# Building the output matrix of a chunked delta rule later, between the splits of a weight stream

## The chip, the cores and the metric

The kernel runs on one core of a Trainium2 chip. The metric is the device time of one execution in microseconds (us); three executions of the kernel before gave 1591.21, 1593.24 and 1593.59 us.

## The reference

One decoder layer for 256 prompt tokens and 8 sequences of 4 sample tokens, everything in fp32. What matters here:

```python
proj = x @ w_in                                  # 2048 -> 11280 columns, split in parts
y_a  = (gB * conv3(gC * h)) @ w_a_out            # mixer A
q, k, v = silu(conv4(q|k|v))                     # mixer B, 8 heads of 128
q, k = l2norm(q), l2norm(k)
# gated delta rule, chunks of 64 tokens, per head:
decay = exp(gcum_i - gcum_j)  where j <= i       # gcum: running sum of g within the chunk
M     = strict_lower(beta * (k k^T) * decay)
T     = inverse(I + M)
attn  = (q k^T) * decay                          # the matrix for the outputs
v_new = T(beta v) - T(beta k exp(gcum)) S
o     = (q exp(gcum)) S + attn v_new
S     = S exp(glast) + (k exp(glast - gcum))^T v_new
y_b   = (rmsnorm(o) * silu(z)) @ w_b_out
x = LN(ALPHA * x + (sigmoid(m_a) * y_a + sigmoid(m_b) * y_b) @ w_o)
x = LN(ALPHA * x + relu(x @ w_up)^2 @ w_down)    # 2048 -> 8192 -> 2048
```

## The kernel before, in words

**The weight stream.** All weights (266 MB) pass once through the core in blocks of 512 KB (`blocks`, some 500 of them). Each block is loaded by SP's queue into a buffer `raw`, split by ACT into a rounded part `hi` (`split_hi`, L194) and by DVE into the rest `lo = raw - hi` (`split_lo`, a subtraction recorded by the helper at L149), and used by PE in 24 matmuls of 288 columns (`matmuls`, L215): for every 128 rows and 128 columns one of the high part of x with `hi`, one of its low part (`xl`, `dl`, `hl`) with `hi`, one of the high part with `lo`. `raw`, `hi` and `lo` have four buffers each. A block's `hi` and `lo` are made three blocks ahead (two in the first ten), and its `raw` is asked for seven ahead, as soon as the `lo` that read the same buffer last is done.

**Order.** There is no scheduler: each engine works in the order in which the program was written. The main loop goes over the blocks; in each it writes the `hi` of block i+3, one step of the side work, `lo` of block i+3, the evacuations that are due (dictionary `due`), and then the 24 matmuls. So DVE and ACT reach the side step of a block in the same order as their splits, and whatever waits in a step has the next splits queued behind it.

**The side work** is a generator, one `yield` per block. `gdn(0)` and then `gdn(1)` run the delta rule for heads 0 to 3 and 4 to 7 (called the first and the second delta rule below). A step's names: `gl`, `glx` are the decays and their split for the running sums; `E` is `decay`; `nr` and `rn` the norms of k and their reciprocals; `nM` (in the buffer `gl`) is -M; `aT` is the matrix for the outputs, `E` times q k^T; `mx` the diagonal 8x8 blocks; `U` the inverse, built from them by a chain of small DVE operations (L1408 to L1416), a transpose, and small 32x32 matmuls (L1399). The decay needs an exponential (L1306) and the norms a root (L1314) on ACT. `kq` products lie in two PSUM tiles of a pool of four (`gtile`) until `nM` and `aT` have read them. Then the chunks c = 0 to 3 follow: L1571 (state times q and k), L1583 (`v`), L1596 and L1599 (new state and outputs), with extra empty steps for the first delta rule. A second generator (`aux`, `sample`) steps along in the same blocks for the sample tokens. POOL's queue loads the sample states of two heads (`states_in(2)`, `states_in(3)`, 512 KB each) in the step that makes `mx`.

**The start.** x comes token by token and is turned by PE transposes, 128 columns at a time; the last quarter of the prompt goes over DVE and POOL instead (`x_turn`, `x_moves`, `x_last`). `x_sample(3)` turns the last quarter of the sample tokens: a transpose put among the matmuls of block 5, a copy on ACT (`xh`), a subtraction on DVE (`xl`). Block 6 is the first that needs that quarter.

**The first down projection** (`mark["down", 0]`, 16 blocks): each pair of blocks ends in `acc += psum` on DVE (`down_evac`), which also frees one of the two PSUM accumulators. In the same blocks pieces of the normalised x are split (`normal`, whose `parts` makes `dl`); they were entered in `due` before the evacuations.

Of the kernel before, what the change touches and what calls it, by code (L numbers as in the profile page):

```python
# [110 lines left out]
def hybrid_kernel(ctx: ExitStack, tc: tile.TileContext, A):  # L111
# [105 lines left out]
    def matmuls(i):  # L217
        gi, r0, k0, first, last = blocks[i]
        if gi.get("by_token"):
            return first_tokens(i, k0)  # L220
        members = gi.get("pair", (gi,))
        if first:
            for m in members:
                m["ps"] = acp.tile([P, 2, 512], F32, tag="acc", name=nm("acc"))
        ps = members[0]["ps"]
        h, l = his.pop(i), los.pop(i)
        ah, al = gi["acts"]()
        n = gi["width"]
        kb = gi["kb"]
        h, l = (u.rearrange("p k c -> p (k c)").rearrange("p (k c) -> p k c", k=kb) for u in (h, l))  # L230
        for k in range(kb):
            xh_, xl_ = ah[:, k0 + k, 0:n], al[:, k0 + k, 0:n]
            st = first and k == 0
            en = last and k == kb - 1
            per = gi["cols"] // P // len(members)
            for u, m in enumerate(members):
                ts = [(m["ps"][:, t, 0:n], slice((per * u + t) * P, (per * u + t + 1) * P)) for t in range(per)]
                both = [(o, c, x) for o, c in ts for x in (xh_, xl_)]
                behind = i == mark["down", 0] + 1 and k > 1
                for o, c, x in both[::2] if behind else both[::2] + both[1::2] if i == 0 else both:  # L240
                    stream(o, h[:, k, c], x, start=st and x is xh_, stop=False)
                for o, c in ts:
                    stream(o, l[:, k, c], xh_, start=False, stop=en and not behind)
                    if fill:
                        fill.pop(0)()
                for o, c, x in both[1::2] if behind else ():
                    stream(o, h[:, k, c], x, start=False, stop=en)
        if last:
            for n, f in enumerate(gi["evac"]):
                at(i + 1 + n, lambda f=f: f(ps))  # L250


    NE, NL = CF_AT["early"], CF_AT["late"]
# [939 lines left out]
    def gdn(G):  # L1193
# [59 lines left out]
        def move_sums(s):  # L1253
            for b in range(2):
                for i in range(4):
                    gps.tensor_copy(red4[64 * s + 32 * b:64 * s + 32 * b + 32, i].rearrange("p (c r) -> p c r", r=2),
                                    ptv[32 * i:32 * i + 32, 1 - s, b])

        for n in range(4):
            for f, hh in ((total, n - 2), (square, n - 1), (turn, n)):  # L1260
                if hh >= 0:
                    f(hh)
            if n != 1 or G == 0:
                yield
        total(2)
        square(3)
        tt(gl, bc(G_["g"][:, :, pr], 64),
           cst("lc").unsqueeze(1).unsqueeze(1).to_broadcast([P, 4, 2, 64]), MUL)
        gps.memset(aT, 0.0)
        glf = gl.rearrange("p c r x -> p (c r x)")  # L1270
        glx = pl.tile([P, 2, 512], F32R, tag="vml", name=nm("glx"))
        act.copy(glx[:, 0], glf)
        yield
        tt(glx[:, 1], glf, glx[:, 0], SUB)
        total(3)
# [27 lines left out]
        act.copy(kr, sp2[:, 0:P])  # L1303
        move_k(gps.tensor_copy, 1, 0)
        yield
        act.activation(Ef, Ef, AF.Exp)  # L1306

        for u, q4, par, r in halves:
            tt(Tm[r, q4], kk2[u][r, :, par], bmid(ident[r, 64 * par:64 * par + 64], 4), MUL)
        dve.tensor_reduce(out=ss[:, 0:8], in_=Tm, axis=mybir.AxisListType.X, op=ADD)  # L1310
        yield
        nr = T([P, 9], "nr")
        rn = T([P, 9], "rn")
        act.activation(nr, ss[:, 0:9], AF.Sqrt, bias=epsc[:, 1:2])  # L1314
        move_sums(0)
        yield
# [7 lines left out]
        stt(nbr, brk, -1.0, rk, MUL, MUL)  # L1324
        nM = T([P, 8, 64], "gl")
        tt(nM, Ef, bc(qc(nbr), 64), MUL)
        tt(Ef, Ef, bc(rn[:, 0:8], 64), MUL)
        for u, q4, par, r in halves:
            tt(nM[r, q4], kk2[u][r, :, par], nM[r, q4], MUL)
        yield  # L1330
        for u, q4, par, r in halves:
            tt(aT[r, q4, 64 - 64 * par:128 - 64 * par], kk2[u][r, :, 1 - par], Ef[r, q4], MUL)

        n8 = sqr[:, 0:64].rearrange("p (q j) -> p q j", q=8)
        u8 = sqr[:, 64:128].rearrange("p (q j) -> p q j", q=8)
        t8 = sqr[:, 128:192].rearrange("p (q j) -> p q j", q=8)
# [58 lines left out]
        def pairs(out, a, b):  # L1395
            for q in range(8):
                for w in range(4):
                    r = slice(32 * w, 32 * w + 32)
                    pe.matmul(out[r, q * 32:q * 32 + 32], a(r, q, w), b[r, q, :], start=True, stop=True)  # L1399

        yield
        n88 = gtile()
        for u in range(2):
# [162 lines left out]
        for c in range(4):  # L1566
            blk, half = c // 2, c % 2
            if c:
                p1 = gtile().rearrange("p (h x) -> p h x", h=4)
                for hh in range(4):  # L1570
                    pe.matmul(p1[:, hh, :], kq[:, hh, c].rearrange("p s x -> p (s x)"), S[:, hh, :],  # L1571
                              start=True, stop=True)
                for hh in range(4):
                    r = rows[hh % 2]
                    stt(v[r, c, hh // 2, :], p1[r, hh, :], G_["neg"][r, c, 2 * G + hh // 2:2 * G + hh // 2 + 1],
                        v[r, c, hh // 2, :], MUL, ADD)
                for par in range(2):
                    r = rows[1 - par]
                    tt(o[r, c], p1[r, par::2, :], bc(G_["egs"][r, c, pr], P), MUL)
                yield  # L1580
            p2 = gtile()
            for p in range(2):
                pe.matmul(p2[:, p * P:(p + 1) * P], U128[:, 2 * c + p, :], v[:, c, p, :], start=True, stop=True)  # L1583
            tt(v[:, c], p2[:, 0:256].rearrange("p (r x) -> p r x", r=2), bc(brk[:, c, :], P), MUL)
            if c == 0:
                kdf = kdec.rearrange("p c r x -> p (c r) x")
                tt(kdf, kdf, bc(qc(kdr), P), MUL)
                dve.tensor_reduce(out=ss[:, 9:17], in_=red4.rearrange("p i n -> p n i"), axis=mybir.AxisListType.X,
                                  op=ADD)
            yield  # L1590
            if c == 0 or G == 0:
                yield
            p3, p4 = [gtile()[:, 0:256].rearrange("p (h c) -> p h c", h=2) for _ in range(2)], gtile()
            for hh in range(4):
                r = rows[hh % 2]
                pe.matmul(p3[hh % 2][:, hh // 2, :], kdec[r, c, hh // 2, :], v[r, c, hh // 2, :],  # L1596
                          start=True, stop=True)
            for p in range(2):
                pe.matmul(p4[:, p * P:(p + 1) * P], aT[:, 2 * c + p, :], v[:, c, p, :], start=True, stop=True)  # L1599
            p4v = p4[:, 0:256].rearrange("p (r x) -> p r x", r=2)  # L1600
            if c == 0:
                for par in range(2):
                    act.copy(S[:, par::2, :], p3[par])
                act.copy(o[:, c], p4v)
            else:
                for hh in range(4):
                    stt(S[:, hh, :], S[:, hh, :], G_["egl"][:, blk, 4 * G + hh, half:half + 1],
                        p3[hh % 2][:, hh // 2, :], MUL, ADD)
                tt(o[:, c], o[:, c], p4v, ADD)
            yield  # L1610
            if G == 0 and c < 2:
                yield
        gps.dma_start(A["new_gdn_prompt"][0, 0, hs].rearrange("h d e -> d h e"), S)
        while not done:
# [113 lines left out]
    for i in range(len(blocks)):  # L1728
# [7 lines left out]
        if i in (1, 3):  # L1736
            a_, s_, b_ = x_fill(i // 2 + 1)
            fill.extend([idle, a_, s_, b_])
        if i == 5:
            fill.extend([idle, idle, lambda: x_sample(3)()])  # L1740
        if i == 6:
            fill.extend([idle, idle, idle, idle, hist_tiles, hist_tiles2])
# [115 lines left out]
```

## Time and profile before

| | before |
|---|---|
| three runs, median (range) | 1593.24 us (1591.21 to 1593.59) |
| the profiled execution's own time | 1591.5 us |
| its span, first to last instruction | 1589.4 us |
| granted TensorE clock | 0.999 |
| PE busy in the span | 1580.8 us |
| DVE busy | 979.2 us |
| ACT busy | 783.6 us |

A row of the timeline has the start in us, the length in us, the engine, the source line, the operation, what it writes and reads, how many instructions the row merges, and in brackets how long the engine sat idle before it and for whom. `SPq` and `POOLq` are issues of transfers. Lengths of neighbouring instructions overlap, since they are pipelined: the step from one start to the next is what an instruction costs its engine.

### The profile page before, as it was taken

To read this page: it belongs to the slowest core of one execution; us is meant where nothing else is said; L and a number is where in the kernel's file an instruction comes from. 1 tells how busy PE (TensorE), PEld (TensorE's weight loads), DVE (VectorE), ACT (ScalarE), POOL (GpSimd) and SP (SyncE) were. 2 spreads that over 40 slices of the span, in tenths; PEclk is the share of its full clock that TensorE was granted. 3 is DMA by queue.
4 is the path that set the end of the run, shared out by engine and by line. 5 is a ranking of instruction groups with operands and counts; after the bars stand their busy time and mean duration, and the time that the engine had idled before them with its cause. 6 is when DMAs were issued, how large, how long until landed. Compare 5 with 4: busy or idle time off the path is not lost.

```text
span 1589.4 us, 31399 instructions
## 1 busy us (share of the span) xinstructions
PE 1580.8 (99%) x13125; PEld 1565.2 (98%) x13125; DVE 979.2 (62%) x1301; ACT 783.6 (49%) x1231; POOL 133.0 (8%) x278
## 2 busy tenths in 40 slices
PE   9999999999999999999999999999999999999998
PEld 8999999999999999999999999999999999999997
DVE  6787788777544455557888755445445544445566
ACT  6786777458533344444456544334334443344454
POOL 1142316133000000000000000000000000000111
PEclk9999999999999999999999999999999999999999
DMA  8666467645755556655555755555555555555653
GB/s 268 176 186 187 135 181 211 188 127 157 224 172 174 173 172 174 177 174 170 168 159 174 235 178 173 173 172 173 172 173 173 174 174 174 174 174 176 188 170 104
DMA packets 273236, 280.42 MB, mean 176 GB/s; under 512 B 13727, under 2 KB 267220, under 8 KB 272832
## 3 DMA queue, kind: packets, MB, share of 16 engines
q1 hardware_dynamic: 269190, 266.06, 55.4%
q0 software_dynamic: 3616, 12.02, 2.8%
q8 instruction: 103, 1.69, 0.5%
q10 hardware_dynamic: 288, 0.33, 0.1%
q14 instruction: 39, 0.32, 0.1%
HBM read 270.88 MB, written 7.48 MB: 175 GB/s over the span
## 4 chain that ended last, share of the span: by engine, by line
PE 93%; ACT 2%; DVE 2%; issue 1%; POOL 0%; DVEq 0%; ACTq 0%
PE acc L215 90%; ACT hi L194 1%; DVE lo L149 1%; DVE w L152 0%; PE g L1399 0%; PE g L1596 0%; PE g L1599 0%; PE g L1571 0%; PE g L1390 0%; PE g L1583 0%; PE g L1549 0%; DVE gl L149 0%; ACT L321 0%; ACT vm L1538 0%; PE g L1094 0%
## 5 line engine op out<-in xcount | busy, mean ns | idle before, releaser
L149 DVE TENSOR_TENSOR lo<-raw,hi 128x1024 fp32r<-128x1024 f32 (+1 forms) x503 | 606.5, 1210 | 512.6 <-ACT hi L194 511.4
L194 ACT CAST hi<-raw 128x1024 fp32r<-128x1024 f32 (+1 forms) x499 | 517.9, 1042 | 654.2 <-PE acc L215 579.0
L215 PE MATMUL acc<-xh,hi 128*128 128x288 f32 x1408 | 385.5, 291 | 0.3 <-ACT xh L1008 0.2
L215 PE MATMUL acc<-xl,hi 128*128 128x288 f32 x1408 | 381.7, 289 | 0.3 <-DVE xl L149 0.3
L215 PE MATMUL acc<-xh,lo 128*128 128x288 f32 x1408 | 294.4, 289 | 0.7 <-DVE lo L149 0.6
L215 PE MATMUL acc<-dl,hi 128*128 128x288 f32 (+1 forms) x1024 | 278.4, 289 | 0.0
L215 PE MATMUL acc<-dh,hi 128*128 128x288 f32 (+1 forms) x1024 | 278.2, 288 | 0.0
L215 PE MATMUL acc<-hh,hi 128*128 128x288 f32 x992 | 268.2, 288 | 0.1
L215 PE MATMUL acc<-hl,hi 128*128 128x288 f32 x992 | 268.2, 288 | 0.0
L215 PEld LDWEIGHTS acc<-xh,hi 128*128 128x128 f32 x1408 | 264.3, 188 | 3.1 <-issue 1.6
L215 PEld LDWEIGHTS acc<-xl,hi 128*128 128x128 f32 x1408 | 264.9, 188 | 1.4 <-DVE xl L149 0.5
L215 PEld LDWEIGHTS acc<-xh,lo 128*128 128x128 f32 x1408 | 222.0, 188 | 1.5 <-DVE lo L149 1.5
L215 PE MATMUL acc<-dh,lo 128*128 128x288 f32 (+1 forms) x1024 | 213.5, 288 | 0.0
L215 PE MATMUL acc<-hh,lo 128*128 128x288 f32 x992 | 206.0, 288 | 0.0
L215 PEld LDWEIGHTS acc<-dl,hi 128*128 128x128 f32 x1024 | 192.4, 188 | 0.0
L215 PEld LDWEIGHTS acc<-dh,hi 128*128 128x128 f32 x1024 | 191.6, 187 | 0.0
L215 PEld LDWEIGHTS acc<-hl,hi 128*128 128x128 f32 x992 | 186.4, 188 | 0.0
L215 PEld LDWEIGHTS acc<-hh,hi 128*128 128x128 f32 x992 | 185.4, 187 | 0.7 <-issue 0.4
L215 PEld LDWEIGHTS acc<-dh,lo 128*128 128x128 f32 x1024 | 161.1, 188 | 0.0
L215 PEld LDWEIGHTS acc<-hh,lo 128*128 128x128 f32 x992 | 155.6, 188 | 0.0
L215 PE MATMUL acc<-mh,hi 128*128 128x288 f32 x256 | 69.2, 288 | 0.0
L215 PE MATMUL acc<-ml,hi 128*128 128x288 f32 x256 | 69.2, 288 | 0.0
(429 smaller groups left out, 1470.9 us busy)
## 6 DMA issues: line engine op xcount, KB each, us to landing
raw<-in_w_in_dram SPq DMA_DIRECT2D x175, 512.0 KB, 4.0
raw<-in_w_up_dram SPq DMA_DIRECT2D x128, 512.0 KB, 3.6
raw<-in_w_down_dram SPq DMA_DIRECT2D x128, 512.0 KB, 3.6
raw<-in_w_o_dram SPq DMA_DIRECT2D x32, 512.0 KB, 4.4
raw<-in_w_a_out_dram SPq DMA_DIRECT2D x16, 512.0 KB, 3.6
raw<-in_w_b_out_dram SPq DMA_DIRECT2D x16, 512.0 KB, 3.6
S<-in_state_gdn_dram POOLq DMA_DIRECT2D x8, 512.0 KB, 5.5
out_dram<-S POOLq DMA_DIRECT2D x8, 512.0 KB, 4.7
```

The lines of the kernel that those rows point to most:

```text
L149: dve.tensor_tensor(out=out, in0=a, in1=b, op=op)
L194: act.copy(his[i][:, k:k + step], raw[i][:, k:k + step])
L215: pe.matmul(out, w, x, **kw)
```

## The change

Five edits, none of which adds or removes an operation of the program's own.

1. `aT` and the product `E * rn` that it needs move from the two steps after the norms to the step just before the matmul with `bo8` (L1404), in both delta rules.
2. The exponential moves one step later, to stand directly ahead of the root.
3. In the second delta rule the decays (`gl` and the high half of `glx`) are made one step earlier.
4. In the first delta rule one empty step moves from behind chunk 1 to between L1571 and L1583 of chunk 3, so that all from the end of chunk 1 to L1571 of chunk 3 comes one block earlier.
5. `x_sample(3)` goes to block 4, and in the first down projection the evacuation stands at the head of its block's `due` list.

```diff
@@ matmuls
             for n, f in enumerate(gi["evac"]):
-                at(i + 1 + n, lambda f=f: f(ps))
+                due.setdefault(i + 1 + n, []).insert(
+                    0 if mark["down", 0] <= i < mark["down", 0] + 16 else 9999, lambda f=f: f(ps))
@@ gdn
+        glf = gl.rearrange("p c r x -> p (c r x)")
+        glx = pl.tile([P, 2, 512], F32R, tag="vml", name=nm("glx"))
+
+        def decays():
+            tt(gl, bc(G_["g"][:, :, pr], 64),
+               cst("lc").unsqueeze(1).unsqueeze(1).to_broadcast([P, 4, 2, 64]), MUL)
+            act.copy(glx[:, 0], glf)
+
         for n in range(4):
             ...
+            if G and n == 3:
+                decays()
             if n != 1 or G == 0:
                 yield
         total(2)
         square(3)
-        tt(gl, bc(G_["g"][:, :, pr], 64), ...)
+        if G == 0:
+            decays()
         gps.memset(aT, 0.0)
-        glf = ...
-        glx = ...
-        act.copy(glx[:, 0], glf)
@@ gdn
         yield
-        act.activation(Ef, Ef, AF.Exp)
-
         for u, q4, par, r in halves:
             tt(Tm[r, q4], kk2[u][r, :, par], bmid(ident[r, 64 * par:64 * par + 64], 4), MUL)
         dve.tensor_reduce(out=ss[:, 0:8], in_=Tm, axis=mybir.AxisListType.X, op=ADD)
         yield
         nr = T([P, 9], "nr")
         rn = T([P, 9], "rn")
+        act.activation(Ef, Ef, AF.Exp)
         act.activation(nr, ss[:, 0:9], AF.Sqrt, bias=epsc[:, 1:2])
@@ gdn
         tt(nM, Ef, bc(qc(nbr), 64), MUL)
-        tt(Ef, Ef, bc(rn[:, 0:8], 64), MUL)
         for u, q4, par, r in halves:
             tt(nM[r, q4], kk2[u][r, :, par], nM[r, q4], MUL)
         yield
-        for u, q4, par, r in halves:
-            tt(aT[r, q4, 64 - 64 * par:128 - 64 * par], kk2[u][r, :, 1 - par], Ef[r, q4], MUL)
...
+        tt(Ef, Ef, bc(rn[:, 0:8], 64), MUL)
+        for u, q4, par, r in halves:
+            tt(aT[r, q4, 64 - 64 * par:128 - 64 * par], kk2[u][r, :, 1 - par], Ef[r, q4], MUL)
         yield
         n88 = gtile()
@@ gdn, chunks
                 yield
+                if G == 0 and c == 3:
+                    yield
             p2 = gtile()
...
-            if G == 0 and c < 2:
+            if G == 0 and c == 0:
                 yield
@@ main loop
-        if i == 5:
+        if i == 4:
             fill.extend([idle, idle, lambda: x_sample(3)()])
```

How the order changes, at three places. First ACT in the first delta rule, before: the exponential stands between a split and the SiLU of v (`vf`, `vfs`), the root one split further down.

```order
L194 CAST hi_1382<-raw_1226 128x1024
L1306 ACT_TABLE_LOAD
L1306 ACTIVATE E_1334<-E_1334 128x512
L321 ACT_TABLE_LOAD
L321 ACTIVATE vf_501<-w_494 128x4x64
L323 ACTIVATE vfs_502<-w_494 128x32
L321 ACTIVATE vf_501<-w_495 128x4x64
L323 ACTIVATE vfs_502<-w_495 128x32
L194 CAST hi_1422<-raw_1262 128x1024
L1314 ACT_TABLE_LOAD
L1314 ACTIVATE nr_1424<-ss_966,epsc 128x9
```

And the same place after:

```order
L194 CAST hi_1382<-raw_1226 128x1024
L322 ACTIVATE vf_501<-w_494 128x4x64
L324 ACTIVATE vfs_502<-w_494 128x32
L322 ACTIVATE vf_501<-w_495 128x4x64
L324 ACTIVATE vfs_502<-w_495 128x32
L194 CAST hi_1421<-raw_1262 128x1024
L1320 ACT_TABLE_LOAD
L1320 ACTIVATE E_1334<-E_1334 128x512
L1321 ACT_TABLE_LOAD
L1321 ACTIVATE nr_1423<-ss_966,epsc 128x9
```

The exponential went behind the next split, and the table load ahead of the SiLU is gone: two loads are left of three.

Second, ACT in the second delta rule, before, where no SiLU lies between the two:

```order
L194 CAST hi_3710<-raw_3568 128x1024
L1306 ACT_TABLE_LOAD
L1306 ACTIVATE E_3671<-E_3671 128x512
L194 CAST hi_3746<-raw_3604 128x1024
L1314 ACT_TABLE_LOAD
L1314 ACTIVATE nr_3748<-ss_3418,epsc 128x9
L194 CAST hi_3787<-raw_3642 128x1024
```

After:

```order
L194 CAST hi_3710<-raw_3568 128x1024
L194 CAST hi_3745<-raw_3604 128x1024
L1320 ACT_TABLE_LOAD
L1320 ACTIVATE E_3671<-E_3671 128x512
L1321 ACT_TABLE_LOAD
L1321 ACTIVATE nr_3747<-ss_3418,epsc 128x9
L194 CAST hi_3787<-raw_3642 128x1024
```

Here the exponential and its table load stand behind the second split instead of ahead of it; as many loads as before.

Third, DVE in the first delta rule from `nM` on, before (the second delta rule has the same order, with its own numbers):

```order
L149 TENSOR_TENSOR gl_1475<-E_1334,nbr_1472 128x512
L149 TENSOR_TENSOR E_1334<-E_1334,rn_1425 128x512
L149 TENSOR_TENSOR gl_1475<-g_1315,gl_1475 64x256 x2
L149 TENSOR_TENSOR gl_1475<-g_1316,gl_1475 64x256 x2
L149 TENSOR_TENSOR lo_1482<-raw_1305,hi_1463 128x1024
L149 TENSOR_TENSOR aT_961<-g_1315,E_1334 64x4x64 x2
L149 TENSOR_TENSOR aT_961<-g_1316,E_1334 64x4x64 x2
L149 TENSOR_TENSOR xt_1333<-gl_1475,cf 128x512
L149 TENSOR_TENSOR lo_1520<-raw_1380,hi_1513 128x1024
```

After, four splits further down, where the product with `rn` and `aT` now stand:

```order
L149 TENSOR_TENSOR mx_1587<-xt_1333,mx_1587 128x512
L149 TENSOR_TENSOR lo_1628<-raw_1510,hi_1625 128x1024
L149 TENSOR_TENSOR w_494<-acc_1485,hs_1483 128x2x256
L149 TENSOR_TENSOR w_494<-acc_1485,hs_1483 128x8x4 x2
L149 TENSOR_TENSOR E_1334<-E_1334,rn_1424 128x512
L149 TENSOR_TENSOR aT_961<-g_1315,E_1334 64x4x64 x2
L149 TENSOR_TENSOR aT_961<-g_1316,E_1334 64x4x64 x2
L149 TENSOR_TENSOR lo_1672<-raw_1541,hi_1663 128x1024
L152 SCALAR_TENSOR_TENSOR w_495<-w_494,hwa,w_495 128x304 x4
L1414 COPY vmh_959<-cf 128x64
```

The five operations passed five splits (`lo` 1481, 1515, 1557, 1597, 1628) and now stand between the gate product `w` of mixer A and the split ahead of the chain that builds `U`.

More of the change, by code (lines that the diff above doesn't have):

```diff
@@ L1266, in gdn @@
         square(3)
-        tt(gl, bc(G_["g"][:, :, pr], 64),
-           cst("lc").unsqueeze(1).unsqueeze(1).to_broadcast([P, 4, 2, 64]), MUL)
+        if G == 0:
+            decays()
         gps.memset(aT, 0.0)
-        glf = gl.rearrange("p c r x -> p (c r x)")
-        glx = pl.tile([P, 2, 512], F32R, tag="vml", name=nm("glx"))
-        act.copy(glx[:, 0], glf)
         yield
```

## The prediction

> **What bounds the kernel now.** I read the page first, then the chain of waits, then PE's timeline, and last those of DVE and ACT at the places where PE waits.
>
> ```profile
> PE 1580.8 (99%) x13125; PEld 1565.2 (98%) x13125; DVE 979.2 (62%) x1301; ACT 783.6 (49%) x1231; POOL 133.0 (8%) x278
> 394.61 325.28 PE acc L215 x2568
> ```
>
> PE is busy for 1580.8 of 1589.4 us. The second row, from the chain of waits, gives its pace without any side work: 325.28 / 2568 = 127 ns for a matmul, so 3.05 us for a block of 24. No edit touches a matmul. The most that can be won is what PE waits, so every wait of PE that lies near an edit has to be priced. From PE's timeline:
>
> ```profile
> 29.18 0.29 PE L215 MATMUL acc<-xh,hi 128*128 128x288 f32 x1
> 29.75 0.40 PE L215 MATMUL acc<-xl,hi 128*128 128x288 f32 x1 [0.28 <-DVE xl L149]
> 113.78 0.40 PE L215 MATMUL acc<-xh,lo 128*128 128x288 f32 x1 [0.25 <-DVE lo L149]
> 117.40 0.39 PE L215 MATMUL acc<-xh,lo 128*128 128x288 f32 x1 [0.31 <-DVE lo L149]
> 120.44 0.29 PE L215 MATMUL acc<-xl,hi 128*128 128x288 f32 x1
> 120.81 0.39 PE L215 MATMUL acc<-xh,lo 128*128 128x288 f32 x1
> 218.59 0.38 PE L1583 MATMUL g<-v,U 128*128 128x128 f32 x1 [0.20 <-DVE v L152]
> 871.82 0.41 PE L215 MATMUL acc<-hh,lo 128*128 128x288 f32 x2
> 872.34 0.37 PE L215 MATMUL acc<-hh,hi 128*128 128x288 f32 x1
> ```
>
> The reader is to see that a wait costs more than the gap in brackets: from 29.18 to 29.75 are 0.57 us where 0.13 would do, so a gap of 0.28 costs 0.44, 0.16 more than it shows. With the same 0.16 the gaps at 113.78 and 117.40 cost 0.41 and 0.47. At 120.81 the step is 0.37 instead of 0.13, a loss of 0.25 (rounded up from unrounded starts). At 218.59 it is about 0.3 (0.20 to 0.36). At 872.34 the second of the pair started at 871.95, so the loss is 0.27. All together 2.1 us, 0.13% of the time: the prize is that small.
>
> **The x of the sample tokens.**
>
> ```profile
> 26.14 1.14 ACT L1054 CAST xh<-xm 128x512 fp32r<-128x512 f32 x2 [0.47 <-POOL xm L1049]
> 28.27 1.23 DVE L149 TENSOR_TENSOR lo<-raw,hi 128x1024 fp32r<-128x1024 f32 x1 [0.18 <-ACT hi L194]
> 29.41 0.28 DVE L149 TENSOR_TENSOR xl<-g,xh 128x128 fp32r<-128x128 f32 x1
> ```
>
> PE waits for the `xl` that ends at 29.69, and that one stood behind the split of 28.27. A block earlier, its copy fits into ACT's idle 0.47 before 26.14, and the subtraction runs with DVE idle. What is late next is the `lo` of block 6: it ends at 29.50, and PE asks for it five matmuls into the block, at 29.18 + 4 x 0.127 = 29.69. Gain 0.44, and no less than 0.25 by that margin if the split slips by the length of the small operation. SP's transfers keep their order.
>
> **The first delta rule.**
>
> ```profile
> 101.85 1.28 ACT L1306 ACT_TABLE_LOAD   x1
> 103.78 1.28 ACT L321 ACT_TABLE_LOAD   x1
> 108.64 0.21 DVE L1318 RECIPROCAL rn<-nr 128x9 f32<-128x9 f32 x1 [0.39 <-ACT nr L1314]
> 110.02 0.69 DVE L149 TENSOR_TENSOR E<-E,rn 128x512 f32<-128x512 f32 x1
> 112.50 1.23 DVE L149 TENSOR_TENSOR lo<-raw,hi 128x1024 fp32r<-128x1024 f32 x1
> 113.76 1.73 DVE L149 TENSOR_TENSOR aT<-g,E 64x256 f32<-64x256 f32 x4
> 121.00 1.05 ACT L194 CAST hi<-raw 128x1024 fp32r<-128x1024 f32 x1 [0.72 <-DMA raw<-in_w_in_dram]
> 122.87 1.22 DVE L149 TENSOR_TENSOR lo<-raw,hi 128x1024 fp32r<-128x1024 f32 x1
> 126.13 1.22 DVE L149 TENSOR_TENSOR lo<-raw,hi 128x1024 fp32r<-128x1024 f32 x1 [1.00 <-ACT hi L194]
> 135.31 0.45 DVE L1416 STREAM_TRANSPOSE U<-U 128x256 f32<-128x256 f32 x1
> 136.18 0.31 PE L1399 MATMUL g<-U,gl 32*32 32x32 f32 x13
> ```
>
> First the root. Without the exponential ACT saves 1.93 us (101.85 to 103.78) and the SiLU's table load of 1.28. It then waits for DVE's last convolution piece, and pays 1.28 and some 0.65 for the exponential behind the next split. By hand the norms come within 0.1 us of 108.6, so DVE starts `rn` as before.
>
> Then the splits. The `lo` of 112.50 loses `E * rn` ahead of it (0.69) and ends at about 113.05; PE's lost 0.41 says that it wanted it at 113.37. The next ones have 0.69 + 1.73 = 2.4 us less ahead of them, against losses of 0.47 and 0.25. All three waits go: gain 1.13 us. The 2.4 us turn up ahead of the `lo` of 126.13, where DVE sat idle for 1.00.
>
> What is late next is `U`. From 108.64 to the end of the transpose (135.76) DVE has 27.12 us, of which 1.00 idle, so 26.12 of work. If that idle is filled by `aT`, `U` ends at 108.7 + 26.1 = 134.8. PE comes 1.13 earlier than 136.18, at 135.05, and needs 0.05 us after the release (113.73 to 113.78). It just fits, with 0.2 to spare. This asks that the weight load which ACT awaited at 121.00 land earlier too: it is asked for when the `lo` of 112.50 ends, 0.7 us sooner, and the sample states of two heads are on their way then. If it landed at the same time, DVE, which reaches the `lo` of 122.87 about 2.35 us sooner and found its `hi` ready for 0.82, would idle for 1.5, and `U` would cost PE 1.3. I take 0, for this reason:
>
> ```profile
> 111.77 1.76 POOL L1201 DMA_DIRECT2D S<-in_state_gdn_dram  x2 [14.04 <-ACT kdec L1250]
> 279.63 1.77 POOL L1201 DMA_DIRECT2D S<-in_state_gdn_dram  x2 [7.10 <-ACT hs L345]
> DMA to landing us min/median/max: 7.1/7.1/7.1
> DMA to landing us min/median/max: 5.4/5.4/5.4
> ```
>
> The two landings are those of the weight loads asked for at 113.75 and at 280.73. The one came 1.1 us after the second state load (issued halfway through the POOL row, at 112.65) and took 7.1 us; the other came 0.2 after it and took 5.4. After the change the first stands at 113.05, 0.4 behind, near the quick one: landing at about 118.5 to 119.
>
> [...]
>
> **The chunks.**
>
> ```profile
> 199.15 0.54 DVE L152 SCALAR_TENSOR_TENSOR w<-w,hw 128x312 f32<-128x312 f32 x1 [2.17 <-ACT w L311]
> 217.08 1.46 DVE L152 SCALAR_TENSOR_TENSOR v<-g,gpt,v 64x128 f32<-64x128 f32 x4
> ```
>
> PE waited at 218.59 for the `v` of 217.08. With an empty step between them it has a block more. The same four operations of chunk 2 go a block earlier, into the idle 2.17 ahead of 199.15. PE has 12 blocks with side matmuls there before and after, so the entries cost the same. Gain 0.3.
>
> **The decays of the second delta rule.**
>
> ```profile
> 91.92 0.72 PE L1285 MATMUL g<-glx,hmr 128*128 128x512 f32 x2
> 263.99 0.96 PE L1285 MATMUL g<-glx,hmr 128*128 128x512 f32 x2
> ```
>
> The same two matmuls take 0.24 more there, because they catch up with DVE's `glx`. A product less ahead of it gives that back: 0 to 0.24, and I take 0.24.
>
> **The down projection.** The evacuation goes ahead of one split of `dl`, which nobody reads before the next up projection. PE's 0.27 at 872.34 goes.
>
> **The second delta rule**, where the same moves cost.
>
> ```profile
> 270.95 1.28 ACT L1306 ACT_TABLE_LOAD   x1
> 272.92 1.05 ACT L194 CAST hi<-raw 128x1024 fp32r<-128x1024 f32 x1
> 275.62 0.21 DVE L1318 RECIPROCAL rn<-nr 128x9 f32<-128x9 f32 x1 [0.39 <-ACT nr L1314]
> 275.96 1.05 ACT L194 CAST hi<-raw 128x1024 fp32r<-128x1024 f32 x1 [0.37 <-PE acc L215]
> 293.13 1.23 DVE L149 TENSOR_TENSOR lo<-raw,hi 128x1024 fp32r<-128x1024 f32 x1 [1.00 <-ACT hi L194]
> 300.30 0.45 DVE L1416 STREAM_TRANSPOSE U<-U 128x256 f32<-128x256 f32 x1
> 300.90 0.28 PE L1399 MATMUL g<-U,gl 32*32 32x32 f32 x10
> ```
>
> Here no SiLU lies between, so no table load is saved. The split of 272.92 cannot go earlier: the next one waited for PE to free its buffer at 275.96, a block of 3.04 later. So ACT idles from 270.93, ends the split at 273.97, and only then runs load, exponential, load, root. Before, these took 275.6 - 270.95 - 1.05 = 3.6 us without the split. The norms come at 277.5, and DVE's `rn` at 277.55, 1.93 later. DVE's work from `rn` to the end of `U` is 300.75 - 275.62 - 1.00 = 24.13, so `U` is there at 301.68 and PE, due at 300.90, starts at 301.73: a new wait of 0.83 us, all of the weight stream behind it. The bounds are 0, if that split finds its buffer free, and 1.7, if its weight load is then 0.9 late as well.
>
> **The sum.** -0.44 - 1.13 - 0.30 - 0.24 - 0.27 + 0.83 = -1.55 us. The profiled execution took 1591.5 us (2.1 of it around the span), so 1590.0. The median of the runs, 1593.24, is 1.7 above it; the same difference gives 1591.7.
>
> **The rivals.** *The second delta rule does not fall behind* (`hi` free earlier, or DVE's work shorter): the whole 2.38 stays, 1590.9. Against it stands the wait for PE at 275.96.
>
> *The weight loads come in behind the state loads in both delta rules, and the kernel gets slower.* Price 1.3 us in the first; in the second the load of 280.73 is asked for 1.2 later, and with 7.1 us would land at 289.0, where its cast ran at 288.16 unhindered (its `lo` is reached half a microsecond sooner than before): 0.9 more. -1.55 + 2.2 gives +0.65: 1593.9. It decides from 119.5 us on in the first (134.8 moves from there on) and from 288 in the second.
>
> *The change does not do what it says:* DVE and ACT are early, but PE then waits for the next thing, a buffer or a load; the gains of 113 to 121 and of the chunks come back as other waits. What stays is -0.44 - 0.24 - 0.27 + 0.83, about 0: 1593.1.
>
> [...]
>
> [...]
>
> **The chances.** The sum 0.58; no lag in the second delta rule 0.13; loads behind the states 0.12; gains taken back 0.14; pause 0.03. A measurement of this kernel tells 0.2%, 3.2 us, from nothing: three runs alone lie 2.4 us apart. No case reaches that by itself; with the runs' spread the second case could (0.10 faster), the last and the third hardly (0.04 slower), and 0.86 stay within. The range takes the runs' own spread below the first two cases (down 2.0 from 1591.7 gives 1589.7, a little less for the second) and the third case above: 1589.4 to 1594.2.
>
> **What would show it.** Right: no gap at 29.7, 113 to 121, 218 and 872; two table loads of three at 101 to 108; PE waiting near 300 for `U` by 0.6 to 1 us, with a new idle of DVE ahead of `rn` of about 2.3. Wrong: no wait at that place; a wait for `U` already at 135, behind a cast that waits for a load; or a new wait of PE before 100.

## The result, and the profile after

The changed kernel takes 1589.03 us (median of 22 runs, 1588.40 to 1591.12), the kernel before 1592.03 in 22 runs (one of them took 4142.74; without it the median is 1591.84). The ratio of the two is 0.9984 with a 95% interval of 0.9977 to 0.9990, so the change takes off 1.6 to 3.7 us. The forecast was 1591.7, with 1589.4 to 1594.2. By that ratio the 1593.24 that it started from become 1590.7; the median of 1589.03 itself lies 0.4 below the low end.

The profiled execution took 1589.15 us, its span 1587.3 instead of 1589.4. The first line of the page, busy time by engine:

```profile
PE 1577.3 (99%) x13125; PEld 1563.1 (98%) x13125; DVE 979.4 (62%) x1301; ACT 782.7 (49%) x1230; POOL 134.0 (8%) x278
```

ACT has one instruction less (1230 against 1231), the table load that is saved. To find 2 us in 1587 I use that PE runs the same 11904 matmuls of the weight stream (L215) in the same order in every kernel here. The time between the starts of two of them is the same within 0.06 us in each trace wherever no kernel differs, so each place can be priced alone. The wait for `U` in the first delta rule is less steady: 4.22 to 4.43 us in the kernels that have the same order there. The table is worked out from the starts in the traces, in us. "start" is matmul 0 to 72, `x` is 144 to 168 (near 29 us), `lo` 740 to 800 (112 to 121), `U1` 900 to 920 (the first delta rule's wait for `U`, near 135), "chunks" 1200 to 1440, "decays" 1700 to 1760, `U2` 2010 to 2020 (the second rule's `U`, near 300), "down" 6300 to 6360, and "rest" all from matmul 72 to the last one. The rows below the second are the experiments.

```
                            start     x    lo    U1  chunks  decays    U2  down     rest
before                      14.48  4.71  9.07  3.41   38.21   10.64  2.15  7.96  1562.09
changed                     13.90  4.17  7.60  4.43   37.46   10.39  2.91  7.60  1560.55
changed, once more          14.79  4.16  7.60  4.22   37.46   10.39  2.91  7.60  1560.30
exponential back            16.14  4.17  7.60  4.24   37.46   10.39  2.91  7.60  1560.35
matrix back                 13.80  4.18  9.17  3.41   37.46   10.39  4.02  7.60  1562.21
states later                14.59  4.16  7.60  3.60   37.44   10.39  2.89  7.60  1559.65
small edits back            15.47  4.73  7.60  4.37   38.20   10.63  2.90  7.97  1562.35
second rule as before       13.91  4.17  7.60  3.59   37.44   10.39  2.15  7.60  1558.91
product, matrix sooner      13.42  4.16  7.60  3.41   37.46   10.39  2.66  7.60  1559.24
product sooner              13.06  4.53  7.60  3.41   37.46   10.39  2.15  7.60  1559.08
warm-up                     13.51  4.56  7.60  4.25   37.46   10.39  2.91  7.60  1560.73
gains together              13.19  4.69  7.60  3.53   37.46   10.39  2.15  7.60  1559.37
```

Behind the start the change is worth 1562.09 - 1560.55 = 1.54 us, where the sum had said 1.55. The terms do not agree as well: 0.54 at `x`, 1.47 at `lo`, 0.75 in the chunks, 0.25 at the decays, 0.36 down, and against them 1.02 at `U1` and 0.76 at `U2`. From PE's timeline after, the places that were clean of waits first, then the two where PE now waits:

```profile
28.67 0.29 PE L215 MATMUL acc<-xh,hi 128*128 128x288 f32 x1
28.79 0.29 PE L215 MATMUL acc<-xl,hi 128*128 128x288 f32 x1
112.35 0.41 PE L215 MATMUL acc<-xh,lo 128*128 128x288 f32 x2
115.39 0.41 PE L215 MATMUL acc<-xh,lo 128*128 128x288 f32 x2
118.43 0.41 PE L215 MATMUL acc<-xh,lo 128*128 128x288 f32 x2
134.69 0.75 PE L1402 MATMUL g<-U,gl 32*32 32x32 f32 x64 [0.94 <-DVE U L1422]
216.25 0.60 PE L1591 MATMUL g<-v,U 128*128 128x128 f32 x4
299.19 0.75 PE L1402 MATMUL g<-U,gl 32*32 32x32 f32 x64 [0.69 <-DVE U L1422]
870.38 0.29 PE L215 MATMUL acc<-hh,hi 128*128 128x288 f32 x1
```

From 112.35 to 115.39 and on to 118.43 are 3.04 us each, one block without a wait. Of the two waits for `U` one had been forecast. What lies behind the other, from the timelines of ACT and DVE:

```profile
104.14 1.28 ACT L1320 ACT_TABLE_LOAD   x1
105.43 0.63 ACT L1320 ACTIVATE E<-E 128x512 f32<-128x512 f32 x1
106.09 1.28 ACT L1321 ACT_TABLE_LOAD   x1
107.72 0.22 DVE L1325 RECIPROCAL rn<-nr 128x9 f32<-128x9 f32 x1 [0.48 <-ACT nr L1321]
119.19 1.05 ACT L194 CAST hi<-raw 128x1024 fp32r<-128x1024 f32 x1 [2.41 <-DMA raw<-in_w_in_dram]
120.27 1.23 DVE L149 TENSOR_TENSOR lo<-raw,hi 128x1024 fp32r<-128x1024 f32 x1 [0.83 <-ACT hi L194]
134.19 0.45 DVE L1422 STREAM_TRANSPOSE U<-U 128x256 f32<-128x256 f32 x1
```

And from the view of the line that loads the weights, the load asked for at 112.1:

```profile
DMA to landing us min/median/max: 7.0/7.0/7.0
```

It takes 7.0 us, against 7.1 before; its cast waits 2.41 us for it, the DVE 0.83 for the cast, and `U` is that much late. And in the second rule:

```profile
271.52 1.28 ACT L1320 ACT_TABLE_LOAD   x1
273.46 1.28 ACT L1321 ACT_TABLE_LOAD   x1
275.10 0.22 DVE L1325 RECIPROCAL rn<-nr 128x9 f32<-128x9 f32 x1 [2.34 <-ACT nr L1321]
298.69 0.45 DVE L1422 STREAM_TRANSPOSE U<-U 128x256 f32<-128x256 f32 x1
```

The idle of 2.34 ahead of `rn`, the 24.04 us from there to the end of `U` and the wait of PE stand as forecast. Whether the late `rn` causes the wait is what the first two runs ask.

### The profile page after: what moved, and what is told of

The parts are those of the page before. It is cut to its first block, busy times and chain, and to the rows that moved or that the text cites. A ratio compares the mean times of both kernels' runs of the same rounds, so it can differ in the third digit from the quotient of the medians.

```text
span 1587.3 us, 31400 instructions
## 1 busy us (share of the span) xinstructions
PE 1577.3 (99%) x13125; PEld 1563.1 (98%) x13125; DVE 979.4 (62%) x1301; ACT 782.7 (49%) x1230; POOL 134.0 (8%) x278
## 4 chain that ended last, share of the span: by engine, by line
PE 93%; DVE 3%; ACT 2%; DMA 1%; issue 1%; SPq 0%; DVEq 0%; ACTq 0%
PE acc L215 89%; DVE lo L149 1%; DMA raw<-in_w_in_dram 1%; DVE w L152 1%; ACT hi L194 1%; PE g L1402 0%; PE g L1577 0%; PE g L1604 0%; PE g L1607 0%; DVE gl L149 0%; PE g L1393 0%; PE g L1555 0%; PE g L1591 0%; DVE vmh L149 0%; DVE aT L149 0%
## 5 line engine op out<-in xcount | busy, mean ns | idle before, releaser
L149 DVE TENSOR_TENSOR lo<-raw,hi 128x1024 fp32r<-128x1024 f32 (+1 forms) x503 | 606.5, 1211 | 511.5 <-ACT hi L194 510.3
L215 PE MATMUL acc<-xh,hi 128*128 128x288 f32 x1408 | 385.1, 291 | 0.8 <-ACT hi L1688 0.4
L215 PE MATMUL acc<-xl,hi 128*128 128x288 f32 x1408 | 380.9, 288 | 0.0
L215 PE MATMUL acc<-xh,lo 128*128 128x288 f32 x1408 | 293.4, 288 | 0.0
L215 PE MATMUL acc<-dl,hi 128*128 128x288 f32 (+1 forms) x1024 | 278.4, 289 | 0.0
L215 PE MATMUL acc<-dh,hi 128*128 128x288 f32 (+1 forms) x1024 | 278.2, 288 | 0.0
L215 PE MATMUL acc<-hh,hi 128*128 128x288 f32 x992 | 268.2, 288 | 0.0
L215 PE MATMUL acc<-hl,hi 128*128 128x288 f32 x992 | 268.2, 288 | 0.0
L215 PEld LDWEIGHTS acc<-xh,hi 128*128 128x128 f32 x1408 | 263.8, 188 | 3.8 <-issue 1.4
L215 PEld LDWEIGHTS acc<-xl,hi 128*128 128x128 f32 x1408 | 264.4, 188 | 0.8
L215 PEld LDWEIGHTS acc<-xh,lo 128*128 128x128 f32 x1408 | 221.6, 188 | 0.2 <-DVE lo L149 0.2
L215 PE MATMUL acc<-dh,lo 128*128 128x288 f32 (+1 forms) x1024 | 213.5, 288 | 0.0
L215 PE MATMUL acc<-hh,lo 128*128 128x288 f32 x992 | 206.0, 288 | 0.0
L215 PEld LDWEIGHTS acc<-dl,hi 128*128 128x128 f32 x1024 | 192.5, 188 | 0.0
L215 PEld LDWEIGHTS acc<-dh,hi 128*128 128x128 f32 x1024 | 191.6, 187 | 0.0
L215 PEld LDWEIGHTS acc<-hl,hi 128*128 128x128 f32 x992 | 186.4, 188 | 0.0
L215 PEld LDWEIGHTS acc<-hh,hi 128*128 128x128 f32 x992 | 185.4, 187 | 0.4 <-issue 0.4
L215 PEld LDWEIGHTS acc<-dh,lo 128*128 128x128 f32 x1024 | 161.1, 188 | 0.0
L215 PEld LDWEIGHTS acc<-hh,lo 128*128 128x128 f32 x992 | 155.6, 187 | 0.0
L215 PE MATMUL acc<-mh,hi 128*128 128x288 f32 x256 | 69.2, 288 | 0.0
L215 PE MATMUL acc<-ml,hi 128*128 128x288 f32 x256 | 69.2, 288 | 0.0
```

The costliest lines, as they stand in the source:

```text
L149: dve.tensor_tensor(out=out, in0=a, in1=b, op=op)
L215: pe.matmul(out, w, x, **kw)
```

## The experiments

**The exponential back in its old place, in both rules.**

```
         yield
+        act.activation(Ef, Ef, AF.Exp)
         for u, q4, par, r in halves:
             tt(Tm[r, q4], ...)
...
-        act.activation(Ef, Ef, AF.Exp)
         act.activation(nr, ss[:, 0:9], AF.Sqrt, bias=epsc[:, 1:2])
```

> The changed kernel with the exponential back in its old place, two steps ahead of the root's step, in both delta rules; everything else as changed. Theory (the later exponential gains nothing in the first delta rule and costs a wait in the second): in the first the norms keep their place, the three waits for `lo` stay gone, and PE's wait for U of about 1.0 us stays; in the second the norms come 1.9 us sooner, DVE's idle of 2.34 ahead of `rn` shrinks to about 0.4, and PE's wait for U of 0.7 goes. So 0.75 us less than the changed kernel's 1589.0: 1588.3. Rival (the moved exponential, not the moved matrix, is what removed the `lo` waits, through the saved table load): the waits near 112 to 119 come back, 1.4 us, and the time is 1589.7 or more.

1589.72 us (0.9989 of before, 0.9980 to 0.9998). That is the time of the rival, but its waits are not there. The `lo` stretch stays at 7.60, so the exponential has no part in the gain of the first rule. But `U2` stays at 2.91 too, and here my theory fell. Rows of DVE, ACT and PE from this run's timeline (its times lie 2.02 us later than the changed kernel's here, 301.21 against 299.19 for PE, most of it from the start):

```profile
275.17 0.22 DVE L1326 RECIPROCAL rn<-nr 128x9 f32<-128x9 f32 x1 [0.39 <-ACT nr L1322]
284.63 1.05 ACT L194 CAST hi<-raw 128x1024 fp32r<-128x1024 f32 x1 [1.99 <-PE acc L215]
285.71 1.23 DVE L149 TENSOR_TENSOR lo<-raw,hi 128x1024 fp32r<-128x1024 f32 x1 [0.58 <-ACT hi L194]
288.80 1.23 DVE L149 TENSOR_TENSOR lo<-raw,hi 128x1024 fp32r<-128x1024 f32 x1 [1.26 <-ACT hi L194]
301.21 0.75 PE L1403 MATMUL g<-U,gl 32*32 32x32 f32 x64 [0.69 <-DVE U L1423]
```

`rn` does come 1.95 us sooner (275.17 - 2.02 = 273.15 against 275.10). The DVE then gives it back: it idles 0.58 and 1.26 ahead of two splits, whose casts wait until PE frees a buffer (for the second cast this trace names nobody; the changed kernel's trace names PE for the same wait of 1.51). From 288.80 on the place of `U` is set by PE's own pace and by what the DVE has to do behind that point, and the matrix, 2.4 us, now lies behind it.

**The matrix back, the exponential as changed.**

```
         tt(nM, Ef, bc(qc(nbr), 64), MUL)
+        tt(Ef, Ef, bc(rn[:, 0:8], 64), MUL)
...
         yield
+        for u, q4, par, r in halves:
+            tt(aT[...], kk2[u][r, :, 1 - par], Ef[r, q4], MUL)
         n8 = sqr[:, 0:64]...
...
-        tt(Ef, Ef, bc(rn[:, 0:8], 64), MUL)
-        for u, q4, par, r in halves:
-            tt(aT[...], kk2[u][r, :, 1 - par], Ef[r, q4], MUL)
         yield
```

> The changed kernel with the matrix aT and the product E * rn back in their old steps in both delta rules, the exponential still beside the root. Theory (DVE's 2.42 us ahead of the splits were what PE waited for): the three `lo` waits of the first rule come back, 1.1 to 1.4 us in all, and its wait for U (1.0) goes, since the DVE has no idle time ahead of U; in the second rule, where the norms are 1.9 us later than before the change, new `lo` waits of 0.5 to 1.5 us show up and the wait for U gets shorter or goes. Time 1589.2 to 1590.5. Rival (the `lo` waits came from the weight loads or from the table loads): no waits near 112 to 119, time 1588 to 1588.5.

1592.08 us, the same as before (1.0002, 0.9993 to 1.0012) and 1.6 above what I had expected at most. The `lo` waits are back (9.17) and `U1` is clean (3.41): in the first rule the moved matrix makes both the gain and the wait. In the second I had the place wrong, since no split was late and `U2` grew to 4.02:

```profile
112.73 0.53 PE L215 MATMUL acc<-xh,lo 128*128 128x288 f32 x2 [0.35 <-DVE lo L149]
116.35 0.53 PE L215 MATMUL acc<-xh,lo 128*128 128x288 f32 x2 [0.31 <-DVE lo L149]
293.05 1.23 DVE L149 TENSOR_TENSOR lo<-raw,hi 128x1024 fp32r<-128x1024 f32 x1 [1.00 <-ACT hi L194]
300.72 0.75 PE L1406 MATMUL g<-U,gl 32*32 32x32 f32 x64 [1.80 <-DVE U L1423]
```

With the run before this makes a square for `U2`: neither moved 2.15, the exponential alone 4.02, the matrix alone 2.91, both 2.91. The late norms cost 1.87 us alone and nothing once the matrix is moved. The moved matrix costs 0.76 alone; where the norms are late it takes 1.11 off (4.02 to 2.91). The row at 293.05 tells why lateness alone is not taken up: the idle of 1.00 that before has at 293.13 is still there. It ends with a cast that stands in ACT's queue behind a copy, and that copy waits for the DVE's own `w`, by 2.62 us in the trace of before (291.84, the cast at 292.06). So this idle moves along when the DVE is late; it is filled by work put into it, as by the matrix in the changed kernel.

**The state loads of the first rule later.**

```
-        states_in(2)
-        states_in(3)
+        if G:
+            states_in(2)
+            states_in(3)
...
         tt(kdr, G_["kd"][:, :, pr], rk, MUL)
+        if G == 0:
+            gps.tensor_copy(T([P, 4, 2], "kdj"), kdr)
+            states_in(2)
+            states_in(3)
```

> The changed kernel with the two later state loads of the first delta rule (512 KB each, on POOL's queue) held back some 6 us: they wait for a small copy of `kdr`, which the DVE computes near 117.2, instead of going out at 110.9 to 112.6. Theory (the weight load asked for at 112.1 stands behind them): it lands in 4 to 5 us instead of 7.1, its cast no longer idles 2.4 us, the DVE's idle of 0.83 goes, U is ready 0.8 us sooner, and PE's wait for U falls from 0.94 to between 0 and 0.2. About 0.85 us less: 1588.2. A weight load asked for near 117.3 takes the 7 us then, and its cast near 124.5 can bear that. Rival (that load is slow for another reason, such as the weight queue itself): it still takes about 7 us and the wait and the time (1589.0) stay.

1588.18 us (0.9979, 0.9969 to 0.9989). The weight load asked for at 112.7, from the same view:

```profile
DMA to landing us min/median/max: 3.5/3.5/3.5
```

Its cast, and PE's matmuls on `U`, from the timelines:

```profile
117.34 1.05 ACT L194 CAST hi<-raw 128x1024 fp32r<-128x1024 f32 x1
134.52 0.75 PE L1407 MATMUL g<-U,gl 32*32 32x32 f32 x64
```

The landing is halved, 7.0 to 3.5 us; the cast waits for no load, and `U1` falls from 4.43 to 3.60. What is left over before's 3.41, 0.19, is the DVE's own work. So the state loads delay the weight load, and that delay is most of what `U1` lost: 0.83 of 1.02 us against the changed kernel's first trace, 0.62 of 0.81 against its second.

**The small edits back**, as they were before:

```
-        if i == 4:
+        if i == 5:
             fill.extend([idle, idle, lambda: x_sample(3)()])
...
-            if G and n == 3:
-                decays()
...
-                if G == 0 and c == 3:
-                    yield
...
-            if G == 0 and c == 0:
+            if G == 0 and c < 2:
                 yield
...
-                due.setdefault(i + 1 + n, []).insert(...)
+                at(i + 1 + n, lambda f=f: f(ps))
```

> The kernel before with the two edits of the delta rules alone (matrix and exponential); the x of the last sample, the decays, the chain's empty step and the order of the down projection's evacuation are as before. Theory (each small edit gains in its own place and PE carries each loss to the end): 0.55 come back near 29.7 us, 0.24 in the decays of the second rule near 264, about 0.75 in the chunks between 190 and 218 and 0.25 near 872, in all 1.8 us over the changed kernel: 1590.8. Rival (PE's later waits for U take up what was lost ahead of them): the waits for U near 135 and 300 shrink by what was lost before them, 0.3 to 0.8 us, and the time is 1590.0 to 1590.5.

1591.79 us (1.0005, 0.9996 to 1.0015), 1.0 above the 1590.8 expected; the kernel before took 1591.49 beside it, and the table puts this run 0.26 over that kernel. Each of the four places returns to before's value, and the waits for `U` keep their size (4.37 and 2.90), against the rival: behind the start the run is 1562.35 - 1560.55 = 1.80 us over the changed kernel. Taken alone, the two delta rule edits thus cost 0.26 against before: 1.47 won at `lo`, 0.96 and 0.75 lost at `U1` and `U2`, within 0.03.

**The second rule as before, the states later.**

```
         yield
+        if G:
+            act.activation(Ef, Ef, AF.Exp)
...
+        if G == 0:
             act.activation(Ef, Ef, AF.Exp)
         act.activation(nr, ss[:, 0:9], AF.Sqrt, bias=epsc[:, 1:2])
...
         tt(nM, Ef, bc(qc(nbr), 64), MUL)
+        if G:
+            tt(Ef, Ef, bc(rn[:, 0:8], 64), MUL)
...
+        if G:
+            for u, q4, par, r in halves:
+                tt(aT[...], kk2[u][r, :, 1 - par], Ef[r, q4], MUL)
         n8 = sqr[:, 0:64]...
...
+        if G == 0:
             tt(Ef, Ef, bc(rn[:, 0:8], 64), MUL)
             for u, q4, par, r in halves:
```

> The changed kernel with the second delta rule's matrix and exponential as before the change (its decays stay a step sooner), and with the two later state loads of the first delta rule held back as in the run on the states. Theory (in the second rule the moved matrix costs PE the wait for U, whatever the exponential does): no wait for U near 300, the step there is the 0.90 us of 64 matmuls, 0.75 less than changed; near 135 the wait stays at 0.1 as with the later states. Time 1588.2 - 0.75 = 1587.4, some 1.6 below the changed kernel. Rival (PE's waits in the second rule come from something behind it, such as the order of its loads): the wait near 300 stays at 0.7 and the time is 1588.2.

1587.88 us (0.9975, 0.9966 to 0.9985). `U2` is 2.15, the value of before, and all behind the start is 0.74 less than with the later states alone (1558.91 against 1559.65): what the second rule costs is the two moves made in it.

**Product and matrix a step sooner** (in the second rule the exponential is back in its old place too, and the matrix goes with the product in that rule alone).

```
         yield
+        if G:
+            act.activation(Ef, Ef, AF.Exp)
...
         tt(mx[:, 1], Xf, mx[:, 0], SUB)
+        tt(Ef, Ef, bc(rn[:, 0:8], 64), MUL)
+        if G:
+            for u, q4, par, r in halves:
+                tt(aT[...], kk2[u][r, :, 1 - par], Ef[r, q4], MUL)
         yield
...
```

> The changed kernel with the second rule's exponential in its old place, and with the product E * rn a step sooner in both rules; in the second rule the matrix aT too. Theory (the DVE idles ahead of a `lo` whose `hi` comes late, and work moved ahead of that idle is free): in the first rule 0.69 of DVE work goes into the idle of 0.83 behind the weight load, and PE's wait for U near 135 falls from 0.94 to about 0.25; in the second 2.4 us of work go ahead of the idle of 1.26 that the run with the old exponential had near 288, and the wait for U of 0.69 goes. Together some 1.4 us less than changed: 1587.6. Rival (U hangs on the norms alone, as predicted, and the place of the matrix does not matter): both waits keep their size.

1587.67 us (0.9979, 0.9970 to 0.9988). In the first rule the wait is gone (3.41), more than the 0.7 forecast. In the second it only fell to 2.66. Its rows, DVE and ACT:

```profile
286.38 1.23 DVE L149 TENSOR_TENSOR lo<-raw,hi 128x1024 fp32r<-128x1024 f32 x1
287.64 1.01 DVE L149 TENSOR_TENSOR w<-acc,hs 128x512 f32<-128x512 f32 x3
288.36 0.32 ACT L360 COPY w<-hwa 128x16 f32<-128x16 f32 x2 [3.22 <-DVE w L149]
288.58 1.05 ACT L194 CAST hi<-raw 128x1024 fp32r<-128x1024 f32 x1
289.66 1.23 DVE L149 TENSOR_TENSOR lo<-raw,hi 128x1024 fp32r<-128x1024 f32 x1 [1.01 <-ACT hi L194]
```

2.4 us were put ahead of an idle of 1.26, so the split behind it is late, and with it `w`, ACT's copy that waits for `w`, and the cast queued behind that copy. The DVE idles 1.01 for this cast. In the changed kernel the matrix had filled that second idle.

**The product alone a step sooner** (the second rule's exponential still in its old place).

> The changed kernel with the second rule's exponential in its old place and the product E * rn a step sooner in both rules; the matrix aT keeps its new step in both. Theory (the DVE has two idles in the second rule, 1.26 ahead of one `lo` and 1.0 ahead of the next; work is free only as far as it fits into the idle it is put ahead of, and the matrix a step sooner overran the first and brought back the second): 0.69 go into the first and 1.73 are set against the second, neither `lo` is late, and PE's wait for U near 300 is 0 to 0.1; near 135 it is gone as in the run before. Time some 1.7 below the changed kernel: 1587.4. Rival (the matrix has to go a step sooner as well): the wait near 300 stays at 0.4 to 0.7.

1587.92 us (0.9981, 0.9972 to 0.9990), `U1` 3.41 and `U2` 2.15: both waits gone with the matrix in its new step. DVE's rows show the two idles, one partly filled, the other closed:

```profile
283.85 0.68 DVE L149 TENSOR_TENSOR E<-E,rn 128x512 f32<-128x512 f32 x1
285.19 1.23 DVE L149 TENSOR_TENSOR lo<-raw,hi 128x1024 fp32r<-128x1024 f32 x1 [0.66 <-ACT hi L194]
287.38 1.72 DVE L149 TENSOR_TENSOR aT<-g,E 64x256 f32<-64x256 f32 x4
289.13 1.23 DVE L149 TENSOR_TENSOR lo<-raw,hi 128x1024 fp32r<-128x1024 f32 x1
```

**More warm-up at the start.**

```
     def second_tile():
+        warm_up(3)
         turns(t0[2:4])
```

> The changed kernel with three more warm-up matmuls on zeros (bf16, 512 columns) on PE ahead of the transposes of the second input tile, where PE waits 1 to 1.5 us for the input near 5.9 us. It adds work and changes nothing else. Theory (the runs differ by how long the first matmuls go at a pitch of 0.24 us instead of 0.13, which follows PE's idle time there): the matmuls after that place go at 0.13 in the profile, and the runs' times lie closer together at the low end, 1588.0 to 1589.3, median 1588.4. Rival (the pitch follows something else): the spread stays at some 2.7 us and the median at 1589.0 or 0.3 above it.

> The changed kernel itself once more, as the control of this batch. Both theories: 1589.0, with PE's waits for U of about 0.9 near 135 and 0.7 near 300, and a first 17 us that differ from run to run by up to 2.5 us.

1588.73 us (0.9981, 0.9973 to 0.9990) in 11 runs from 1588.25 to 1589.08, a spread of 0.83. The changed kernel beside it on the same chip took 1589.39 (0.9987, 0.9978 to 0.9996), 11 runs from 1588.25 to 1589.90, and 2.72 us in the 22 runs of the result. PE's rows near the wait for the second input tile, first of the run with the exponential back (start 16.14), then of the changed kernel (13.90), then with the warm-up (13.51):

```profile
7.59 0.69 PE L1020 MATMUL g<-cf,xr 128*128 128x128 f32 x2 [1.48 <-DMA xr<-in_x_prompt_dram]
8.32 0.68 PE L215 MATMUL acc<-xh,hi 128*128 128x288 f32 x2
12.54 0.68 PE L215 MATMUL acc<-xl,hi 128*128 128x288 f32 x2
```

```profile
6.88 0.44 PE L1020 MATMUL g<-cf,xr 128*128 128x128 f32 x2 [0.99 <-DMA xr<-in_x_prompt_dram]
7.28 0.42 PE L215 MATMUL acc<-xh,hi 128*128 128x288 f32 x2
```

```profile
5.56 0.82 PE L947 MATMUL g<-warm 128*128 128x512 bf16 x3
6.94 0.44 PE L1020 MATMUL g<-cf,xr 128*128 128x128 f32 x2 [0.56 <-DMA xr<-in_x_prompt_dram]
7.35 0.42 PE L215 MATMUL acc<-xh,hi 128*128 128x288 f32 x2
```

A pair of 0.68 us is two matmuls 0.24 apart, a pair of 0.42 two at 0.13. With the matmuls on zeros the stretch of ten matmuls at 0.24, which starts at 8.32 in the first of these traces, is not there. The changed kernel's trace shows none either, nor do four others without the warm-up, so this trace alone tells nothing. The spread does: the low end of the times is 1588.25 in both kernels, and the high end 1589.08 with the warm-up against 1589.90, which I take for the slow starts that are missing.

**The gains together**: the second rule as before, the product of the first rule a step sooner, the warm-up.

> The parts that gained, together: the changed kernel with the second rule's matrix and exponential as before the change, the product E * rn of the first rule a step sooner (its state loads stay where they were), and the three warm-up matmuls at the start. Theory: no wait for U in either rule (1.0 and 0.75 less than changed), and a start that varies little: 1588.7 - 1.75 = 1587.0, runs within about 1 us of each other. Rival (the gains take from one another, since what PE wins in the first rule it waits for in the second): 1587.5 or more.

1587.14 us, 1586.86 to 1587.45 in 8 runs; 0.9974 of before (0.9964 to 0.9984). Beside the changed kernel's 0.9984 the interval overlaps; the table shows what is gained, `U1` 3.53 and `U2` 2.15. The `x` stretch gives back 0.5 (4.69, near 29 us); I take it for the `lo` that the prediction named as late next there, after a quicker start.

## Why the prediction was right, and where it was not

The sum was right to 0.01 us behind the start, but by errors that cancel, so the closeness is luck.

- **The x of the sample:** 0.54 where 0.44 was taken. Mechanism and place as forecast; the 0.1 is the matmul behind, see the next point. Undone together with the other small edits, 0.56 come back at its own place. The three kernels with the warm-up or the quickest start lose 0.36 to 0.52 there again (4.53 to 4.69 against 4.17), which fits the `lo` that it named as late next.
- **The three `lo` waits:** all gone, 1.47 instead of 1.13. What the prices left out is the matmul behind the one that waited: it starts 0.23 us later instead of 0.13. The rows of the run with the matrix back show it, where the two on `lo` take 0.53 instead of 0.41. Three times 0.11 and the 1.13 make 1.46. That run shows the cause too.
- **`U` in the first rule:** here a step failed. "I take 0" rested on the weight load landing at 118.5 to 119 because it is asked for 0.4 us behind the second state load instead of 1.1. It took 7.0 us all the same, and the wait cost 1.02 (0.81 in the second trace), inside the bound of 1.3 that I had kept. A wait for `U` at 135 behind a cast that waits for a load was one of my own signs of being wrong. With the state loads held back 0.19 stayed, though the DVE idles nowhere from `rn` to `U`: the 0.2 to spare were not there either, with PE 0.34 sooner than forecast at the splits (1.47 instead of 1.13).
- **The chunks:** 0.75 instead of 0.3. The mechanism was right, the term too small. By the starts in the traces, the four matmuls on `v` and the side matmul that follows took 1.35 us in before, from the stream matmul at 217.80 to the next one, and 1.01 from that at 201.83; the same five take 0.81 at 216.12 after the change. So chunk 2's `v` was late as well, without a gap that the timeline prints.
- **The decays** 0.25 and **the down projection** 0.36, against 0.24 and 0.27.
- **`U` in the second rule:** 0.76 against 0.83, with the named rows all there, and yet the named cause does not hold. I had laid the wait to the norms that come 1.93 us later. The square above shows that they are hidden by the matrix's move, and that the matrix costs 0.76 by itself. The 24.13 us of DVE work from `rn` on were counted rightly, with the matrix in the idle of 1.00; what failed is the lower bound of 0 for norms that come in time, where 0.76 stayed. Worked out afterwards, and not tested: with the exponential back, the split at 288.80 is the paced one. PE is 0.45 us ahead of the kernel before there, so the same pace would have put it at 289.25 in before. There the DVE came to it at 289.87, 0.62 late (the row of before: `289.87 1.22 DVE L149 TENSOR_TENSOR lo<-raw,hi 128x1024 fp32r<-128x1024 f32 x1`). Without 2.42 us ahead of it DVE can win back those 0.62 and no more, and behind it it loses the 2.42 less the second idle of 1.00: 2.42 - 1.00 - 0.62 = 0.80. Two routes gave nearly the same number, so the number could not tell them apart.
- **The rivals:** no run shows the pause behind table loads that has 0.03 of the chances; 105.43 and 106.09 follow within 0.03 us of what is ahead. The loads behind the states came true in the first rule alone; in the second the load took 5.6 us against 5.4. "Gains taken back" came true in part: 1.78 of 3.37 us went into the waits for `U`.
- **The start** was in no term. It is 0.58 of the profiled difference, and it differs between two runs of one kernel as much (13.90 and 14.79). The medians lie 3.0 us apart in the 22 runs and 2.2 in the later batch (1591.55 and 1589.39), where the places behind the start give 1.54. The rest is not explained by any term, and no run here tells whether the change itself shortens the start.

## What to carry to other kernels

Work taken off a busy engine ahead of a deadline has to be followed to the next deadline: here 2.4 us of DVE work freed three splits in the first rule and made `U` late in both. Before moving work, look for idle of that engine, and put into each no more than fits; 0.69 and 1.73 us in two idles cost nothing, 2.4 in the first made the next split late and brought the second back. Ask of each idle what ends it: one that ends with PE's pace takes up lateness (here 0.58 and 1.26 us, against norms 1.95 us later), one that ends with an answer to the engine's own earlier work moves along with it (here the 1.00 us, there before and with the matrix back). And when a number comes out as forecast, undo its cause alone, since two causes that hide one another can give the same number.

## What the runs showed of the hardware

The runs of one kernel differ by some 3 us (1590.46 to 1593.59 before, one far outlier aside), and in the traces the differences between runs of like kernels lie in the first 16 us: between 13.06 and 16.14 us for the same 72 matmuls, while any stretch behind them that no kernel touches repeats within 0.06. The pitch there is 0.24 us for some matmuls and 0.13 for the rest, and the column of the granted clock shows 1.00 in both of these windows:

```profile
8.00:12.00 4.00, 4.00 (x19) 3.98 (x18) 1.09 (x3) 1.35 (x4) 0.00 (x0) 1.00 1.01 360
8.00:12.00 4.00, 3.87 (x30) 3.37 (x28) 2.96 (x7) 2.09 (x6) 0.00 (x0) 1.00 1.03 370
```

These are the windows of 8 to 12 us, the run with the exponential back and that with the warm-up. The count behind PE's busy time is 19 and 30 matmuls in 4 us; the clock is the column ahead of the last two, which are of DMA. Five traces have a stretch of nine to eleven matmuls at 0.24 between 7 and 10.7 us, and their starts are 14.48 to 16.14; the other seven, two of them with the warm-up, have steps of that length only singly there, and starts of 13.06 to 13.91. The two kernels with the warm-up spread over 0.83 and 0.59 us in 11 and 8 runs, the nine sets of runs of the changed kernel and its variants without it over 1.61 to 2.91. So the pitch goes from 0.24 to 0.13 us at a granted clock of 1.00, and the times lie closer together with the warm-up; what sets the pitch no run here shows.

The weight load delayed by state loads on another queue was the costliest surprise behind the start. In the changed kernel's trace the weight load asked for at 112.1 moved nothing until 114.3. The state loads moved 0.24, 0.04, 0.21, 0.24 and 0.03 MB in the microseconds from 114 to 119, the weight loads 0.05, 0.29, 0.13, 0.05 and 0.27: in the microsecond from 115 on, between the two state loads of 512 KB, the weights had the larger part, and the load that ACT's cast waits for landed at 119.1, when the state loads moved nothing any more. In the trace of before, the weight load asked for at 113.75 moved nothing until 117.4, when the two state loads had moved 1.00 of their 1.05 MB, and it landed at 120.9. So in both traces the state loads moved by themselves for a while as the weight load stood, but the two give no one length for it. What the delay is worth is measured by the landing of 3.5 us with the states held back, against 7.0; why the weight load stands so long stays open.
